# A hybrid decoder layer on one core: the gate, and q beside k, projected in 512-column blocks

## The chip, the cores and the metric

The kernel runs on one core of a Trainium2 chip. The metric is the device time of one execution in microseconds (us). The core's engines are named as in the profile: PE (matmul), PEld (its weight loads), DVE (VectorE), ACT (ScalarE), POOL (GpSimd) and SP (the queue that issues most transfers).

## The reference

One layer over 512 tokens of width 1024, all float32:

```python
h = rms_norm(x, norm_mix_w)
proj = h @ w_in                       # 1024 x 5664
z, xbc, dt_raw, q, k, v, f_raw = jnp.split(proj, [...], axis=-1)
y_ssd = ssd_mixer(xbc, z, dt_raw, ...)        # Mamba-2 scan, 16 heads, 2 groups, 4 chunks of 128 tokens
y_fox = fox_mixer(q, k, v, f_raw, ...)        # forgetting attention, 16 heads of 64, q and k normed per head
x = x + concat([y_ssd, y_fox]) @ w_out        # 2048 x 1024
hf = rms_norm(x, norm_ffn_w)
x = x + conv_gated_mlp(hf, w_up, ..., w_down) # 1024 x 5632, causal conv, silu gate, 2816 x 1024
```

In `ssd_mixer` the result of the scan is multiplied by silu(z), the gate, and normed per group of 512 columns. z, q, k and v have 1024 columns each.

## The kernel before

Every float32 matmul is done as three: each operand is split into a high part and a low part, and `mm3` adds high*high, high*low and low*high into one PSUM tile. `load_split` brings 128x1024 weights (512 KB, tile `wraw`, by SP), casts them on ACT to the high part `wh` (line 105) and subtracts on DVE or POOL for the low part `wl` (line 106). The table `LOW_PART` says which of the two engines does it for which block ("d" DVE, "p" POOL; a block without an entry goes to POOL). There are five `wraw` buffers and three of `wh` and of `wl`.

The normed input stands in SBUF as `xh` and `xl`, features on the partitions. The xBC columns are projected by `feature_tile` (weights stationary, 512 tokens moving; outputs called g and j in the trace). z, q, k and v are projected by `token_block`: 128 tokens of `xh` or `xl` are the stationary operand and 256 columns of the weights move. One call makes 256 output columns for all four token blocks, in two PSUM tiles of 512 columns (two token blocks side by side), with two loads of weights, each used for all four token blocks and then let go. That is 8 k-tiles x 4 token blocks x 3 = 96 matmuls of 256 columns a call. z takes two calls for each of two groups, q, k and v one call each for each of four head groups: 4 + 12 = 16 calls and 1536 matmuls, which the trace calls pq.

PSUM has three banks for such tiles (`bank`, pool pg), four for others (`mbank`), and one for po.

After a z call ACT reads each token block's 256 columns twice (a scaled copy to `gz`, line 392, and a tanh, line 393), and DVE multiplies. After a q or k call ACT makes a scaled copy `tok` (line 478) and a square (line 480), DVE sums the squares per head (line 481), POOL takes the power -1/2 for the norm (line 124), and DVE multiplies all of `tok` (line 486).

`ssd_scan` goes through four chunks of 128 tokens for each group. Per chunk: load and exponentiate the decay matrix `sc` (eight exponentials on ACT, line 427), multiply by C*B, make the output y and the next state, then multiply by the gate, norm, transpose (yT, line 464) and split y into `msh` and `msl`. Scan, and the steps of the attention heads (`fox_qk`, `fox_probs`, `fox_values`, 16 heads), are traced under high priority; the projections and output projections (`out_proj`, trace name po) fill in between. The list `fillers` gives at which head they are traced: q and k of group 1 at head 0, of group 2 at head 4, of group 3 at head 8, each used two heads later.

A scheduler orders the instructions of every engine ahead of time from priority, order of tracing and readiness in its own model of time; on the chip every queue then runs in that fixed order.

Behind the attention come the second norm, the up projection (trace name up, 44 feature tiles of 24 matmuls), and the down projection, seven block products with tiles called Y, X and Z. These use the same `wraw`, `wh` and `wl` buffers; in the down projection one of the operands (`oxh`) lies in the place of `xh`.

Of the kernel before, what the change touches and what calls it, by code (L numbers as in the profile page):

```python
# [8 lines left out]
F32 = mybir.dt.float32  # L9
# [47 lines left out]
def tile_hybrid_layer(  # L57
# [7 lines left out]
    wqkv: bass.AP,  # L65
# [34 lines left out]
    def load_split(src, sub=None):  # L100
        r = wp.tile([P, 1024], F32, tag="wraw", name="wraw", bufs=5)
        nc.sync.dma_start(r, src)
        h = wp.tile([P, 1024], F32R, tag="wh", name="wh", bufs=3)
        l = wp.tile([P, 1024], F32R, tag="wl", name="wl", bufs=3)
        act.copy(h, r)  # L105
        (sub or dve).tensor_tensor(out=l, in0=r, in1=raw(h), op=ALU.subtract)  # L106
        return h, l
# [55 lines left out]
    first = [wp.tile([P, 1024], F32R, tag=t, name=t, bufs=3) for t in ("wh", "wl")]  # L163
# [158 lines left out]
    def token_block(src, key="tb", behind=None):  # L322
        tiles = [bank("pq") for _ in range(2)]
        for kh in range(2):
            h, l = load_split(src[kh], sub=low_part(key))
            for b in range(2):
                for j in range(4):
                    k = 4 * kh + j
                    for c in range(2):
                        tb = 2 * b + c  # L330
                        s = slice(tb * P, (tb + 1) * P)
                        mm3(
                            tiles[b][:, c * 256 : (c + 1) * 256], xh[:, k, s], xl[:, k, s],
                            h[:, j * 256 : (j + 1) * 256], l[:, j * 256 : (j + 1) * 256],
                            k == 0 and c == 0, k == NK - 1, grouped=False,
                        )
                if behind is not None:
                    behind(2 * kh + b)
        return tiles

    def ssd_proj(g):
# [41 lines left out]
        for half in range(2):  # L383
            tiles = token_block(
                wz[2 * g + half], "z%d" % g,
                lambda piece: to_tokens(*late.pop(0)) if 4 * half + piece in (1, 3, 5 if g else 6) else None,
            )
            for tb in range(NTB):
                o = tiles[tb // 2][:, (tb % 2) * 256 : (tb % 2 + 1) * 256]
                dst = gz[tb][:, half * 256 : (half + 1) * 256]  # L390
                th = pss.tile([P, 256], F32, tag="th", name="th", bufs=2)
                act.activation(dst, o, AF.Copy, scale=rhalf[:, tb : tb + 1])
                act.activation(th, o, AF.Tanh, scale=rhalf[:, tb : tb + 1])
                dve.scalar_tensor_tensor(out=dst, in0=th, scalar=1.0, in1=dst, op0=ALU.add, op1=ALU.mult)
# [8 lines left out]
    def ssd_scan(g, x_tok, bT, cT, b_tok, gz):  # L403
# [5 lines left out]
        state = None  # L409
        for c in range(NTB):  # L410
# [5 lines left out]
            pool.tensor_tensor(out=heads(xdt), in0=heads(x_tok[c]), in1=per_head(tokS[:, 0, c, hs]), op=ALU.mult)  # L416
            if c < NTB - 1:
                dte = pss.tile([P, 2, HPG], F32, tag="dte", name="dte", bufs=2)
                dve.tensor_sub(dte[:, 0, :], last, tokS[:, 1, c, hs])
                dve.tensor_copy(dte[:, 1, :], last)  # L420
                act.activation(dte, dte, AF.Exp)
# [8 lines left out]
            dve.tensor_mul(sc, sc, cb[:, None, :P].broadcast_to([P, HPG, P]))  # L430
            yd = mbank("yd")
# [11 lines left out]
            if c < NTB - 1:  # L443
                dve.tensor_mul(heads(xdt), heads(xdt), per_head(dte[:, 0, :]))
                st = mbank("st")
                pe.matmul(st, b_tok[:, c, :], xdt, start=True, stop=True)
                new = pss.tile([P, 512], F32, tag="state", name="state", bufs=2)
                if state is None:
                    dve.tensor_copy(new, st)
                else:  # L450
                    pool.tensor_tensor(out=heads(new), in0=heads(state), in1=per_head(dte[:, 1, :]), op=ALU.mult)
                    dve.tensor_add(new, st, new)
                state = new
            dve.tensor_mul(y, y, gz[c])
# [4 lines left out]
            dve.scalar_tensor_tensor(  # L459
                out=y, in0=y, scalar=ss, in1=nwb, op0=ALU.mult, op1=ALU.mult  # L460
            )
# [5 lines left out]
            dve.tensor_sub(ml[:, :, s], tv, raw(mh[:, :, s]))  # L467
        return [(mh[:, j, :], ml[:, j, :]) for j in range(4)]
# [3 lines left out]
    def qk_proj(gi, t):  # L472
        tiles = token_block(wqkv[gi, t], "qk%d" % gi)
        tok = pa.tile([P, NTB, 256], F32, tag="tok", name="tok", bufs=4)
        ms = pa.tile([P, 16], F32, tag="ms", name="ms", bufs=2)
        for tb in range(NTB):
            o = tiles[tb // 2][:, (tb % 2) * 256 : (tb % 2 + 1) * 256]
            act.activation(tok[:, tb, :], o, AF.Copy, scale=r[:, tb : tb + 1])
            sq = pa.tile([P, 256], F32, tag="sq", name="sq", bufs=2)
            act.activation(sq, o, AF.Square, scale=r[:, tb : tb + 1])  # L480
            dve.tensor_reduce(
                out=ms[:, tb * 4 : tb * 4 + 4], in_=sq.rearrange("p (a b) -> p a b", b=HD), op=ALU.add, axis=AX.X
            )
        rsqrt(ms, ms, 1.0 / HD, 16)
        tv = tok.rearrange("p t (h d) -> p (t h) d", d=HD)
        dve.tensor_mul(tv, tv, ms[:, :, None].broadcast_to([P, 16, HD]))
        return tok

    def v_proj(gi):
        tiles = token_block(wqkv[gi, 2], "v%d" % gi)  # L490
# [137 lines left out]
    def project(g):  # L628
        qk[g] = [qk_proj(g, 0), qk_proj(g, 1)]
# [60 lines left out]
    nw = pa.tile([P, D], F32, tag="tok", name="nw", bufs=4)  # L690
    nc.sync.dma_start(nw, norm_ffn_w.to_broadcast([P, D]))
    for half in range(2):
        c = slice(half * 512, (half + 1) * 512)
        ks = slice(half * 4, half * 4 + 4)
        for tb in range(NTB):
            s = slice(tb * P, (tb + 1) * P)
            with urgent():
                xw = pa.tile([P, 512], F32, tag="tok", name="xw", bufs=4)
                (dve if (half, tb) == (1, 3) else pool).tensor_tensor(out=xw, in0=x2[:, tb, c], in1=nw[:, c], op=ALU.mult)
                t = mbank("hT")  # L700
                for j in range(4):
                    pe.transpose(t[:, j * P : (j + 1) * P], xw[:, j * P : (j + 1) * P], ident)
                tv = t.rearrange("p (j f) -> p j f", j=4)
                act.copy(hh[:, ks, s], tv)
                dve.tensor_sub(hl[:, ks, s], tv, raw(hh[:, ks, s]))
# [27 lines left out]

    def load_unit(q, u):
        rw = wp.tile([P, 1024], F32, tag="wraw", name="wraw", bufs=5)
# [23 lines left out]
    def up_proj(fs, cuts):  # L759
        ws = [load_split(wup[f]) for f in fs]  # L760
# [172 lines left out]
def _lay_out(i, np):  # L933
# [6 lines left out]
    def taps(v):  # L940
# [23 lines left out]
        "wz": w_in[:, 0:1024].reshape(2, 4, 128, 4, 256).transpose(3, 0, 2, 1, 4).reshape(4, 2, 128, 1024),  # L964
        "wxbc": _feature(w_in[:, 1024:2560], np),
        "wqkv": w_in[:, 2576:5648].reshape(2, 4, 128, 3, 4, 256).transpose(4, 3, 0, 2, 1, 5).reshape(4, 3, 2, 128, 1024),
# [29 lines left out]
```

## Time and profile before

| | |
|---|---|
| median of 3 runs | 812.52 us (810.81 to 813.75) |
| profiled execution, its own time | 812.5 us |
| its span in the trace | 810.7 us |
| PE busy | 800.7 us |
| DVE, ACT, POOL busy | 608.0, 437.7, 257.0 us |

The span is what the trace covers; 1.8 us of the execution's time lie around it. A matmul's end in the trace is modelled, and matmuls overlap, so the spacing of their starts says more than their durations. Engines other than PE run beside it.

### The profile page before, as it was taken

What the parts mean: (1) busy time and instruction counts of PE and PEld (TensorE: products, weight loads), DVE (VectorE), ACT (ScalarE), POOL (GpSimd) and SP (SyncE); (2) the same over time, 40 slices, a digit from 0 to 9 for tenths busy, and PEclk for the clock granted to TensorE, in tenths of its full rate; (3) what the DMA queues carried; (4) which work ended last, traced back from release to release, by engine and by line L of the source; (5) the groups of instructions that cost most, each with busy time, mean ns of one, the idle gap of its engine ahead of it and who ended that gap; (6) DMA issues with size and microseconds to landing.
All of it is one profiled execution on the core that took longest, in us unless ns stands there. A gap on an engine that the chain in (4) does not pass through costs nothing.

```text
span 810.7 us, 12402 instructions
## 1 busy us (share of the span) xinstructions
PE 800.7 (99%) x4591; PEld 697.2 (86%) x4591; DVE 608.0 (75%) x992; ACT 437.7 (54%) x835; POOL 257.0 (32%) x263
## 2 busy tenths in 40 slices
PE   8999999999999999999999999999999999999997
PEld 6899889988999999998888888888888888888886
DVE  4696898576579999998896867676667666777844
ACT  7466555543376977575664464344434433556531
POOL 0003344642265454234301423333322333133120
PEclk9999999999999999999999999999999999999999
DMA  9524222331343333334231263322332233299982
GB/s 326 207 94 135 104 104 80 118 130 52 105 131 104 105 106 117 105 108 127 66 89 69 78 183 104 103 86 96 105 103 83 100 103 89 84 252 196 215 190 92
DMA packets 31404, 98.22 MB, mean 121 GB/s; under 512 B 4016, under 2 KB 5104, under 8 KB 31344
## 3 DMA queue, kind: packets, MB, share of 16 engines
q1 hardware_dynamic: 27456, 85.38, 32.5%
q0 software_dynamic: 3456, 11.54, 8.0%
q8 instruction: 36, 0.59, 0.3%
q10 hardware_dynamic: 432, 0.52, 0.2%
q14 instruction: 24, 0.20, 0.1%
HBM read 91.56 MB, written 2.20 MB: 116 GB/s over the span
## 4 chain that ended last, share of the span: by engine, by line
PE 87%; DVE 4%; DMA 3%; POOL 2%; issue 2%; ACT 1%; SPq 0%; DVEq 0%; POOLq 0%
PE up L112 30%; PE pq L112 19%; PE po L112 10%; PE Y L112 6%; PE X L112 4%; PE Z L112 4%; PE g L112 3%; PE o L602 2%; PE pT L588 2%; PE j L112 1%; PE yd L433 1%; DMA sc<-cs_d 1%; PE S L562 1%; PE S L561 1%; DVE xs L375 1%
## 5 line engine op out<-in xcount | busy, mean ns | idle before, releaser
L105 ACT CAST wh<-wraw 128x1024 fp32r<-128x1024 f32 x103 | 108.4, 1052 | 134.3 <-PE up L112 78.6
L112 PE MATMUL pq<-wh,xl 128*128 128x256 f32 x512 | 147.5, 288 | 0.0
L112 PE MATMUL pq<-wh,xh 128*128 128x256 f32 x512 | 147.4, 288 | 0.0
L112 PE MATMUL pq<-wl,xh 128*128 128x256 f32 x512 | 146.2, 285 | 0.0
L112 PE MATMUL up<-hl,wh 128*128 128x512 f32 (+1 forms) x368 | 140.0, 381 | 0.0
L112 PE MATMUL up<-hh,wh 128*128 128x512 f32 (+1 forms) x368 | 139.9, 381 | 0.0
L112 PE MATMUL up<-hh,wl 128*128 128x512 f32 (+1 forms) x368 | 139.7, 380 | 0.0
L106 DVE TENSOR_TENSOR wl<-wraw,wh 128x1024 fp32r<-128x1024 f32 x86 | 110.2, 1281 | 25.3 <-ACT wh L105 21.3
L112 PEld LDWEIGHTS pq<-wh,xh 128*128 128x128 f32 x512 | 97.6, 191 | 2.0 <-issue 1.4
L112 PEld LDWEIGHTS pq<-wh,xl 128*128 128x128 f32 x512 | 97.6, 191 | 1.4 <-issue 1.2
L112 PEld LDWEIGHTS pq<-wl,xh 128*128 128x128 f32 x512 | 97.6, 191 | 1.3 <-issue 0.7
L112 PEld LDWEIGHTS up<-hl,wh 128*128 128x128 f32 x368 | 69.2, 188 | 13.4 <-issue 0.2
L112 PEld LDWEIGHTS up<-hh,wh 128*128 128x128 f32 x368 | 69.1, 188 | 13.2 <-issue 0.2
L112 PEld LDWEIGHTS up<-hh,wl 128*128 128x128 f32 x368 | 69.2, 188 | 13.1
L790 DVE TENSOR_TENSOR up<-up,R 128x512 f32<-128x512 f32 x44 | 30.3, 691 | 59.5 <-PE up L112 59.5
L795 DVE SCALAR_TENSOR_TENSOR ua<-up,pc,ua 128x511 f32<-128x511 f32 (+1 forms) x88 | 66.3, 758 | 1.4
L106 POOL TENSOR_TENSOR wl<-wraw,wh 128x1024 fp32r<-128x1024 f32 x17 | 42.1, 2474 | 59.8 <-ACT wh L105 56.2
L567 ACT ACTIVATE prob<-prob,nm 128x128 f32<-128x128 f32 (+1 forms) x64 | 35.8, 561 | 27.7 <-DVE nm L563 27.5
L751 ACT CAST wh<-T 128x1024 fp32r<-128x1024 f32 (+1 forms) x30 | 29.3, 976 | 36.9 <-PE Z L112 15.3
L752 DVE TENSOR_TENSOR wl<-T,wh 128x1024 fp32r<-128x1024 f32 (+1 forms) x30 | 33.8, 1134 | 19.2 <-ACT wh L751 18.8
L548 POOL TENSOR_SCALAR bias<-cum,tokS 128x256 f32<-128x256 f32 (+1 forms) x32 | 25.9, 818 | 67.9 <-DVE nm L563 59.5
L805 POOL TENSOR_TENSOR ua<-ua 128x512 f32<-128x512 f32 x11 | 15.0, 1364 | 92.6 <-DVE ua L795 92.6
(236 smaller groups left out, 1836.6 us busy)
## 6 DMA issues: line engine op xcount, KB each, us to landing
wraw<-in_wup_dram SPq DMA_DIRECT2D x44, 512.0 KB, 3.3
wraw<-in_wqkv_dram SPq DMA_DIRECT2D x24, 512.0 KB, 3.3
T<-in_wdown_dram POOLq DMA_DIRECT2D x20, 512.0 KB, 7.5
wraw<-in_wout_dram SPq DMA_DIRECT2D x16, 512.0 KB, 3.3
wraw<-in_wxbc_dram SPq DMA_DIRECT2D x11, 512.0 KB, 3.7
T<-in_wdown_dram SPq DMA_DIRECT2D x10, 512.0 KB, 5.9
wraw<-in_wdown_dram SPq DMA_DIRECT2D x10, 512.0 KB, 3.7
wraw<-in_wz_dram SPq DMA_DIRECT2D x8, 512.0 KB, 4.5
```

The costliest lines, as they stand in the source:

```text
L105: act.copy(h, r)
L106: (sub or dve).tensor_tensor(out=l, in0=r, in1=raw(h), op=ALU.subtract)
L112: ins = pe.matmul(o, a, b, start=start and n == 0, stop=stop and n == 2, **kw)
L548: (dve if qb == 2 else pool).tensor_scalar(out=b, in0=cum[:, :n], scalar1=-1.0, scalar2=edge, op0=ALU.mult, op1=ALU.add)
L567: act.activation(p, p, AF.Exp, scale=-1.0, bias=nm[:, qb : qb + 1], accum_out=sm[:, qb : qb + 1])
L588: pe.transpose(t[:, w : w + P], prob[:, o : o + P], ident)
L602: pe.matmul(cols[:m], v[:, kb, lh, vc], pt[:, s], start=kb == 0 and n == 0, stop=kb == NTB - 1, skip_group_check=True,)
L751: act.copy(h[:, :n], src[:, :n])
L752: dve.tensor_tensor(out=l[:, :n], in0=src[:, :n], in1=raw(h[:, :n]), op=ALU.subtract)
L790: dve.tensor_mul(xp, o, R2)
L795: dve.scalar_tensor_tensor(out=a[:, s:], in0=xp[:, : SEQ - s], scalar=pc[:, cw + 2 - s : cw + 3 - s], in1=a[:, s:], op0=ALU.mult, op1=ALU.add,
L805: pool.tensor_tensor(out=k, in0=k, in1=val, op=ALU.mult)
```

## The change

- A new `wide_block` replaces `token_block` for z and for q with k: 512 columns of weights move past each stationary 128 tokens (all 512 z columns of a group; 256 of q beside 256 of k). It makes two passes, each over two token blocks, one PSUM tile of 512 columns per token block. Its four loads are split once in the first pass and held for the second. v stays in `token_block`.
- What reads the results does so once per token block with 512 columns in place of twice with 256. The two norms of q and k follow when the whole block is done. `sq` has one buffer of 512 columns for two of 256.
- `wh` and `wl` get a fourth buffer, in pool pa, taken by every fourth load; `wraw` has three buffers for five, except in the down projection, where two more lie in pool pb. The up projection uses the three `wh` and `wl` of wp alone.
- In `ssd_scan`, the loading and the scores of chunk c+1 are traced ahead of gate, norm and transposes of chunk c.
- Tiles `nw` and `xw` of the second norm move to places in pool pf. The weights in memory are laid out for the new blocks.

```diff
         taken[key] = n + 1
         return dve if order[n % len(order)] == "d" else pool
 
-    def load_split(src, sub=None):
-        r = wp.tile([P, 1024], F32, tag="wraw", name="wraw", bufs=5)
+    loads = [0]
+
+    def load_split(src, sub=None, four=True):
+        r = wp.tile([P, 1024], F32, tag="wraw", name="wraw", bufs=3)
         nc.sync.dma_start(r, src)
-        h = wp.tile([P, 1024], F32R, tag="wh", name="wh", bufs=3)
-        l = wp.tile([P, 1024], F32R, tag="wl", name="wl", bufs=3)
+        where = pa if four and loads[0] % 4 == 3 else wp
+        loads[0] += 1
+        h = where.tile([P, 1024], F32R, tag="wh", name="wh", bufs=3 if where is wp else 1)
+        l = where.tile([P, 1024], F32R, tag="wl", name="wl", bufs=3 if where is wp else 1)
         act.copy(h, r)
         (sub or dve).tensor_tensor(out=l, in0=r, in1=raw(h), op=ALU.subtract)
         return h, l
...
 
     px_ctx = ExitStack()
     px = px_ctx.enter_context(tc.tile_pool(name="px", bufs=1))
-    first = [wp.tile([P, 1024], F32R, tag=t, name=t, bufs=3) for t in ("wh", "wl")]
+    first = [pa.tile([P, 1024], F32R, tag=t, name=t, bufs=1) for t in ("wh", "wl")]
     wdt = px.tile([P, NK, 64], F32R, tag="wdt", name="wdt")
...
         act.activation(eacs, tokS[:, 1, :, 0:16], AF.Exp)
         nc.sync.dma_start(dsk, ssd_d[0:1, :].to_broadcast([P, SSD_HEADS]))
 
-    def token_block(src, key="tb", behind=None):
+    def token_block(src, key="tb"):
         tiles = [bank("pq") for _ in range(2)]
         for kh in range(2):
             h, l = load_split(src[kh], sub=low_part(key))
...
                             h[:, j * 256 : (j + 1) * 256], l[:, j * 256 : (j + 1) * 256],
                             k == 0 and c == 0, k == NK - 1, grouped=False,
                         )
+        return tiles
+
+    def wide_block(src, key, use, behind=None):
+        ws = []
+        for b in range(2):
+            tiles = [bank("pw") for _ in range(2)]
+            for kq in range(4):
+                if b == 0:
+                    ws.append(load_split(src[kq], sub=low_part(key)))
+                h, l = ws[kq]
+                for j in range(2):
+                    k = 2 * kq + j
+                    for c in range(2):
+                        s = slice((2 * b + c) * P, (2 * b + c + 1) * P)
+                        cols = slice(j * 512, (j + 1) * 512)
+                        mm3(tiles[c], xh[:, k, s], xl[:, k, s], h[:, cols], l[:, cols], k == 0, k == NK - 1)
                 if behind is not None:
-                    behind(2 * kh + b)
-        return tiles
+                    behind(4 * b + kq)
+            for c in range(2):
+                use(2 * b + c, tiles[c])
 
...
             dve.scalar_tensor_tensor(out=dst, in0=xp, scalar=1.0, in1=dst, op0=ALU.add, op1=ALU.mult)
             if j < 10:
                 late.append((j, dst))
-        for half in range(2):
-            tiles = token_block(
-                wz[2 * g + half], "z%d" % g,
-                lambda piece: to_tokens(*late.pop(0)) if 4 * half + piece in (1, 3, 5 if g else 6) else None,
-            )
-            for tb in range(NTB):
-                o = tiles[tb // 2][:, (tb % 2) * 256 : (tb % 2 + 1) * 256]
-                dst = gz[tb][:, half * 256 : (half + 1) * 256]
-                th = pss.tile([P, 256], F32, tag="th", name="th", bufs=2)
-                act.activation(dst, o, AF.Copy, scale=rhalf[:, tb : tb + 1])
-                act.activation(th, o, AF.Tanh, scale=rhalf[:, tb : tb + 1])
-                dve.scalar_tensor_tensor(out=dst, in0=th, scalar=1.0, in1=dst, op0=ALU.add, op1=ALU.mult)
+
+        def gate(tb, o):
+            th = tmp("t", "th")
+            act.activation(gz[tb], o, AF.Copy, scale=rhalf[:, tb : tb + 1])
+            act.activation(th, o, AF.Tanh, scale=rhalf[:, tb : tb + 1])
+            dve.scalar_tensor_tensor(out=gz[tb], in0=th, scalar=1.0, in1=gz[tb], op0=ALU.add, op1=ALU.mult)
+
+        wide_block(
+            wz[g], "z%d" % g, gate,
+            lambda piece: to_tokens(*late.pop(0)) if piece in (1, 3, 5 if g else 6) else None,
+        )
         return x_tok, bT, cT, b_tok, gz
...
         hs = slice(g * HPG, (g + 1) * HPG)
         nwb = pss.tile([P, 512], F32, tag="nwb", name="nwb", bufs=1)
         nc.sync.dma_start(nwb, ssd_norm_w[0:1, g * 512 : (g + 1) * 512].to_broadcast([P, 512]))
-        state = None
-        for c in range(NTB):
+        def scores(c):
             s = slice(c * P, (c + 1) * P)
             sc = pss.tile([P, HPG, P], F32, tag="sc", name="sc", bufs=2)
             nc.sync.dma_start(sc, cs_d[None, c * 32 + g * HPG : c * 32 + (g + 1) * HPG, :].to_broadcast([P, HPG, P]))
             last = sc[:, :, P - 1]
             xdt = pss.tile([P, 512], F32, tag="xdt", name="xdt", bufs=2)
             pool.tensor_tensor(out=heads(xdt), in0=heads(x_tok[c]), in1=per_head(tokS[:, 0, c, hs]), op=ALU.mult)
+            dte = None
...
             cb = mbank("cb")
             pe.matmul(cb[:, :P], bT[:, s], cT[:, s], start=True, stop=True)
             dve.tensor_mul(sc, sc, cb[:, None, :P].broadcast_to([P, HPG, P]))
+            return sc, xdt, dte
+
+        def chunk(c, state, sc, xdt, dte):
+            s = slice(c * P, (c + 1) * P)
             yd = mbank("yd")
...
                     pool.tensor_tensor(out=heads(new), in0=heads(state), in1=per_head(dte[:, 1, :]), op=ALU.mult)
                     dve.tensor_add(new, st, new)
                 state = new
+            return y, state
+
+        def gated_norm(c, y):
+            s = slice(c * P, (c + 1) * P)
             dve.tensor_mul(y, y, gz[c])
             ss = pss.tile([P, 1], F32, tag="ss", name="ss", bufs=2)
             t = tmp("yt", "yt")
             act.activation(t, y, AF.Square, accum_out=ss)
             rsqrt(ss, ss, 1.0 / 512, 1)
-            dve.scalar_tensor_tensor(
-                out=y, in0=y, scalar=ss, in1=nwb, op0=ALU.mult, op1=ALU.mult
-            )
+            dve.scalar_tensor_tensor(out=y, in0=y, scalar=ss, in1=nwb, op0=ALU.mult, op1=ALU.mult)
             tp = mbank("yT")
             for j in range(4):
                 pe.transpose(tp[:, j * P : (j + 1) * P], y[:, j * P : (j + 1) * P], ident)
             tv = tp.rearrange("p (j f) -> p j f", j=4)
             act.copy(mh[:, :, s], tv)
             dve.tensor_sub(ml[:, :, s], tv, raw(mh[:, :, s]))
+
+        state, ahead = None, scores(0)
+        for c in range(NTB):
+            y, state = chunk(c, state, *ahead)
+            if c < NTB - 1:
+                ahead = scores(c + 1)
+            gated_norm(c, y)
         return [(mh[:, j, :], ml[:, j, :]) for j in range(4)]
...
-    def qk_proj(gi, t):
-        tiles = token_block(wqkv[gi, t], "qk%d" % gi)
-        tok = pa.tile([P, NTB, 256], F32, tag="tok", name="tok", bufs=4)
-        ms = pa.tile([P, 16], F32, tag="ms", name="ms", bufs=2)
-        for tb in range(NTB):
-            o = tiles[tb // 2][:, (tb % 2) * 256 : (tb % 2 + 1) * 256]
-            act.activation(tok[:, tb, :], o, AF.Copy, scale=r[:, tb : tb + 1])
-            sq = pa.tile([P, 256], F32, tag="sq", name="sq", bufs=2)
+    def qk_proj(gi):
+        tok = pa.tile([P, 2, NTB, 256], F32, tag="tok", name="tok", bufs=2)
+        ms = pa.tile([P, 2, NTB, 4], F32, tag="ms", name="ms", bufs=2)
+
+        def take(tb, o):
+            ov = o.rearrange("p (t f) -> p t f", t=2)
+            act.activation(tok[:, :, tb, :], ov, AF.Copy, scale=r[:, tb : tb + 1])
+            sq = pa.tile([P, 512], F32, tag="sq", name="sq", bufs=1)
             act.activation(sq, o, AF.Square, scale=r[:, tb : tb + 1])
             dve.tensor_reduce(
-                out=ms[:, tb * 4 : tb * 4 + 4], in_=sq.rearrange("p (a b) -> p a b", b=HD), op=ALU.add, axis=AX.X
+                out=ms[:, :, tb, :], in_=sq.rearrange("p (t a b) -> p t a b", t=2, b=HD), op=ALU.add, axis=AX.X
             )
-        rsqrt(ms, ms, 1.0 / HD, 16)
-        tv = tok.rearrange("p t (h d) -> p (t h) d", d=HD)
-        dve.tensor_mul(tv, tv, ms[:, :, None].broadcast_to([P, 16, HD]))
-        return tok
+
+        wide_block(wqk[gi], "qk%d" % gi, take)
+        for t in range(2):
+            mt = ms[:, t].rearrange("p a b -> p (a b)")
+            rsqrt(mt, mt, 1.0 / HD, 16)
+            tv = tok[:, t].rearrange("p t (h d) -> p (t h) d", d=HD)
+            dve.tensor_mul(tv, tv, mt[:, :, None].broadcast_to([P, 16, HD]))
+        return tok[:, 0], tok[:, 1]
 
     def v_proj(gi):
-        tiles = token_block(wqkv[gi, 2], "v%d" % gi)
+        tiles = token_block(wv[gi], "v%d" % gi)
...
 
     hh = pxt.tile([P, NK, SEQ], F32R, tag="xh", name="hh")
     hl = pxt.tile([P, NK, SEQ], F32R, tag="xl", name="hl")
-    nw = pa.tile([P, D], F32, tag="tok", name="nw", bufs=4)
+    nw = pf.tile([P, 1280], F32, tag="bias", name="nw", bufs=2)[:, :D]
     nc.sync.dma_start(nw, norm_ffn_w.to_broadcast([P, D]))
     for half in range(2):
         c = slice(half * 512, (half + 1) * 512)
...
         for tb in range(NTB):
             s = slice(tb * P, (tb + 1) * P)
             with urgent():
-                xw = pa.tile([P, 512], F32, tag="tok", name="xw", bufs=4)
+                xw = pf.tile([P, 512], F32, tag="osum" if tb % 2 else "cum", name="xw", bufs=2)
...
     def part(q, u):
         return wdown[q, :, UNITS[u][0] * 512 : UNITS[u][1] * 512]
 
+    raws = [0]
+
     def load_unit(q, u):
-        rw = wp.tile([P, 1024], F32, tag="wraw", name="wraw", bufs=5)
+        where = wp if raws[0] % 5 < 3 else pb
+        raws[0] += 1
+        rw = where.tile([P, 1024], F32, tag="wraw", name="wraw", bufs=3 if where is wp else 2)
         nc.sync.dma_start(rw[:, 0 : (UNITS[u][1] - UNITS[u][0]) * 512], part(q, u))
         return rw
...
     R2 = pu.tile([P, SEQ], F32, tag="R2", name="R2")
 
     def up_proj(fs, cuts):
-        ws = [load_split(wup[f]) for f in fs]
+        ws = [load_split(wup[f], four=False) for f in fs]
         os = [bank("up") for _ in fs]
...
-        "wz": w_in[:, 0:1024].reshape(2, 4, 128, 4, 256).transpose(3, 0, 2, 1, 4).reshape(4, 2, 128, 1024),
+        "wz": w_in[:, 0:1024].reshape(4, 2, 128, 2, 512).transpose(3, 0, 2, 1, 4).reshape(2, 4, 128, 1024),
         "wxbc": _feature(w_in[:, 1024:2560], np),
-        "wqkv": w_in[:, 2576:5648].reshape(2, 4, 128, 3, 4, 256).transpose(4, 3, 0, 2, 1, 5).reshape(4, 3, 2, 128, 1024),
+        "wqk": w_in[:, 2576:4624].reshape(4, 2, 128, 2, 4, 256).transpose(4, 0, 2, 1, 3, 5).reshape(4, 4, 128, 1024),
+        "wv": w_in[:, 4624:5648].reshape(2, 4, 128, 4, 256).transpose(3, 0, 2, 1, 4).reshape(4, 2, 128, 1024),
```

## Rows read from the trace of the kernel before

**Rows 1.** The page's part 1: span, busy time (share), instructions.
```profile
span 810.7 us, 12402 instructions
...
PE 800.7 (99%) x4591; PEld 697.2 (86%) x4591; DVE 608.0 (75%) x992; ACT 437.7 (54%) x835; POOL 257.0 (32%) x263
```
**Rows 2.** The page's part 2: busy tenths and granted PE clock in 40 slices.
```profile
PE   8999999999999999999999999999999999999997
...
PEclk9999999999999999999999999999999999999999
```
**Rows 3.** The page's part 4: the chain that ended last, by engine.
```profile
PE 87%; DVE 4%; DMA 3%; POOL 2%; issue 2%; ACT 1%; SPq 0%; DVEq 0%; POOLq 0%
```
**Rows 4.** Waits of PE behind its start: line, releaser, us in total, times, longest.
```profile
PE S L561 <- DMA ks<-ks: 1.2, 2, 0.7
...
PE yT L464 <- DVE y L459: 0.6, 1, 0.6
PE xT L352 <- ACT x_tok L358: 0.5, 1, 0.5
...
PE po L112 <- DVE x L258: 0.3, 1, 0.3
```
**Rows 5.** The chain in order of time, unbroken matmul stretches: start, us, what, count.
```profile
145.53 10.43 PE pq L112 x87
156.62 3.83 PE pq L112 x32
...
366.30 9.81 PE po L112 x42
...
475.24 225.78 PE up L112 x996
...
730.97 15.01 PE Z L112 x66
```
**Rows 6.** Groups by form, one of three alike: count, busy us, mean ns, idle before.
```profile
L112 PE MATMUL pq<-wh,xl 128*128 128x256 f32 x512 | 147.5, 288 | 0.0
```
**Rows 7.** Timeline of PE behind transposes, eight starts apart: start, us, what.
```profile
103.35 0.40 PE L112 MATMUL g<-xh,wl 128*128 128x512 f32 x1
...
105.20 0.39 PE L112 MATMUL g<-xl,wh 128*128 128x512 f32 x1
```
**Rows 8.** Groups by form: readers of PSUM on ACT, and two DVE steps of q and k.
```profile
L590 ACT CAST ph<-pT 128x512 fp32r<-128x512 f32 x32 | 17.8, 585 | 6.9 <-PE pT L588 5.7 <-PE o L602 1.0
...
L478 ACT ACTIVATE tok<-pq,r 128x256 f32<-128x256 f32 x32 | 15.1, 472 | 4.2 <-PE pq L112 4.0
...
L486 DVE TENSOR_TENSOR tok<-tok,ms 128x1024 f32<-128x1024 f32 x8 | 13.7, 1710 | 0.5 <-POOL ms L124 0.4
...
L481 DVE TENSOR_REDUCE ms<-sq 128x4 f32<-128x256 f32 x32 | 12.9, 414 | 5.1 <-ACT sq L480 4.8
```
**Rows 9.** Groups by form: the two steps of a split, and where DVE or POOL does it.
```profile
L106 DVE TENSOR_TENSOR wl<-wraw,wh 128x1024 fp32r<-128x1024 f32 x86 | 110.2, 1281 | 25.3 <-ACT wh L105 21.3 <-PE rbc L145 3.8
L105 ACT CAST wh<-wraw 128x1024 fp32r<-128x1024 f32 x103 | 108.4, 1052 | 134.3 <-PE up L112 78.6 <-PE po L112 22.0 <-issue 7.3
...
L106 POOL TENSOR_TENSOR wl<-wraw,wh 128x1024 fp32r<-128x1024 f32 x17 | 42.1, 2474 | 59.8 <-ACT wh L105 56.2 <-issue 2.9 <-POOL ss L124 0.7
```
**Rows 10.** The page's part 6: a load of weights, KB, us to landing.
```profile
wraw<-in_wqkv_dram SPq DMA_DIRECT2D x24, 512.0 KB, 3.3
```
**Rows 11.** Stretches of the attention: us, PE, PEld, DVE, ACT, POOL busy, clock, DMA, GB/s.
```profile
260.00:300.00 40.00, 39.92 (x326) 38.93 (x325) 37.48 (x94) 34.30 (x81) 19.53 (x27) 1.00 0.38 113
...
430.00:459.00 29.00, 28.69 (x147) 23.20 (x145) 19.73 (x30) 9.79 (x15) 10.59 (x8) 1.00 0.23 74
```
**Rows 12.** The chain in order of time: exponentials of a scan, and a norm of q or k.
```profile
79.62 2.44 ACT sc L427 x8
...
253.88 2.93 POOL ms L124
256.83 3.41 DVE tok L486
```

More of the change, by code (lines that the diff above doesn't have):

```diff
@@ L64, in tile_hybrid_layer @@
     wxbc: bass.AP,
-    wqkv: bass.AP,
+    wqk: bass.AP,
+    wv: bass.AP,
     wout: bass.AP,
@@ L628, in project @@
     def project(g):
-        qk[g] = [qk_proj(g, 0), qk_proj(g, 1)]
+        qk[g] = qk_proj(g)
     def project_v(g):
```

## The prediction

> **What bounds the kernel now.** I read the page's busy shares first: PE is busy 800.7 of 810.7 us, DVE 75%, ACT 54% [rows 1]. Busy PE alone would say little, since the ends of matmuls are modelled, so the slices come next: PE is at 9 in all but the first and last of them, and the granted clock stands at its upper level, 2.4 GHz, throughout [rows 2]. The chain that ended last gives PE 87% of the span [rows 3]. And the waits of PE behind its start sum to 1.2 + 0.6 + 0.5 + 0.3 = 2.6 us [rows 4]. So one queue, PE's, sets the time nearly everywhere; what counts is how far apart its matmuls start, and the other engines count only where they would make PE wait. A matmul taken off PE, or made cheaper there, comes off the end; less work elsewhere does not.
>
> **What a matmul costs.** Unbroken stretches of the chain give the spacing. 256 columns (pq): 10.43 / 87 = 0.1199 us and 3.83 / 32 = 0.1197, so 0.1198. 512 columns (up): 225.78 / 996 = 0.2267 [rows 5]. At 2.4 GHz, 256 and 512 columns alone would take 0.1067 and 0.2133 us; each matmul carries some 13 ns beside its columns. Two of 256 take 0.2396 us, one of 512 takes 0.2267.
>
> **The change, step by step.**
>
> Step 1, the matmuls. z is 4 calls of the old block, q and k 8: 12 x 96 = 1152 of the 1536 pq matmuls [rows 6] go, 1152 x 0.1198 = 138.0 us. 576 of 512 columns come. No 512-column matmul with `xh` stationary and weights moving is in the trace, so I bound it. Below: 0.2267, as in up, and as in the down projection's Z, whose stationary operand lies in the place of `xh` and whose weights move (15.01 / 66 = 0.2274) [rows 5]. Above: 0.2336, from the output projection, also token blocks against moving weights (9.81 / 42) [rows 5]. The sum is 130.6 us below and 134.5 above; the gain is 7.4 or 3.5. Between them lies g just behind transposes, where the sequence has been broken: 8 starts in 105.20 - 103.35 = 1.85 us, 0.2313 each [rows 7]. I take 0.2267 for the half that runs in long stretches (z and the first q/k block, 288 matmuls, 65.3 us) and 0.2313 for the other three q/k blocks, which the attention heads break up (288, 66.6 us): 131.9, a gain of 6.1 us.
>
> Step 2, reading the results. 16 + 16 readings of z and 32 + 32 of q and k by ACT, at some 472 ns, become 48 of 512 columns. The nearest row, a 512-column cast out of PSUM, took 585 ns [rows 8]. ACT goes from some 45 to some 28 us. The 32 sums of squares on DVE at 414 ns become 16 of 414 to 828 ns: 0 to 6.6 us less. Neither engine sets the end, so I count nothing.
>
> Step 3, banks. There are still three banks, but a pass now ends with both its tiles 3 matmuls apart. The next pass writes its first tile in the third bank and its second in the bank of the first tile just finished. From that tile's last matmul to the first one that wants its bank there are 6 matmuls, 6 x 0.2267 = 1.36 us; two ACT readings take 2 x 0.585 = 1.17 [rows 8]. This fits if ACT is free, and the second pass has other work ready: all its weights are split already, so the first tile's 24 matmuls (5.4 us) can go ahead. I count nothing; the price without that cover is the third rival.
>
> Step 4, weights. In a first pass a load serves 12 matmuls, 2.7 us, where it served 48 of 256 columns, 5.8 us, before; in a second pass none is needed. A buffer comes free every 2.7 us of the second pass, so the first is free 8.2 us before the block ends. A cast takes 1.05 and the low part 1.28 on DVE or 2.47 on POOL [rows 9], 2.3 to 3.5 us together: hidden for three buffers, and the fourth is wanted only 8.2 us into the next block. The landing, 3.3 us [rows 10], is hidden while three raw buffers run ahead. A feature tile of the up projection lasts 24 x 0.2267 = 5.4 us, so three raw buffers suffice there too. If this cover were gone, one late split at each of the six wide blocks would cost up to 6 x 3.5 = 21 us; nothing in the rows asks for it.
>
> Step 5, the norms of q and k. They come in one piece when a block ends: the power on POOL took 2.93 us and the multiplication on DVE 3.41 in one place of the chain [rows 12], where its mean is 1.71 [rows 8]. Now two of each stand there. They are used two heads later, and PE has v and output projections to fill with. Counted at nothing; the second rival prices it.
>
> Step 6, the scan. The scores of the next chunk move ahead of gate and norm of this one on ACT (the eight exponentials took 2.44 us [rows 12]), DVE and POOL; SP's order of loads does not change, as the norm issues none. yT may come later, but only the output projection wants it, and that is traced behind the q/k block. The two waits of PE that this could remove are 0.6 and 0.5 us [rows 4], and it could add the like: nothing.
>
> Step 7, `nw` and `xw` in other places: their buffers are let go when heads 14 and 15 are done, before x2 is. Nothing.
>
> Sum: 812.5 us (the profiled execution, equal to the median; its span is 1.8 less) - 6.1 = 806.4.
>
> **A rule that speaks against it.** The rows say some 13 ns per matmul beside its columns [rows 5]. The Trainium skill (TensorE: Matmul & The Clock Gate, "Wait — 56ns, not 53.3ns?") puts that fixed cost at about 2.5 ns; an estimate from its figure is 2.5 ns for each pair merged, 576 x 2.5 = 1.4 us, and the kernel would end at 811.1. The trace does not agree where stretches are long; its nearest approach is the output projection, below.
>
> **Rivals.**
>
> First, the cost goes with the columns: the new matmuls run at the output projection's 0.2336 [rows 5], nearly twice the 0.1198 of half the width. Gain 3.5, time 809.0, and with one or two new microseconds of waiting no change that can be measured. For it: operands of the same kind, and many short stretches. Against: Z, with the same place stationary, took 0.2274. The skill's rule of the paragraph above points the same way. 0.14.
>
> Second, the attention cannot use what PE saves. DVE is busy 37.48 of 40 us from 260 to 300, where q and k of group 1 are projected, though only 19.73 of 29 at the end [rows 11]. The fox half of the gain, 288 x (0.2396 - 0.2313) = 2.4 us, goes, giving 808.8; if each of three blocks also shows one more multiplication at its mean of 1.71 us [rows 8], 5.1 in all, 813.9. 0.14.
>
> Third, and slower: the bank of step 3. Six blocks have 12 ends of passes. With one cast of 1.05 us [rows 9] ahead of the two readings on ACT, which takes its queue in order, the bank is free 1.17 + 1.05 - 1.36 = 0.86 us late; behind eight exponentials [rows 12], 2.3 us. 12 x 0.86 = 10.3 us gives 816.7. It decides from 6.1 / 12 = 0.5 us per end. For it: the room shrinks from 48 matmuls of 256 columns, 5.8 us. Against: in 16 blocks PE never waited for ACT to read a projection [rows 4], and the order is laid out with readiness in view. 0.15.
>
> **How the numbers follow.** My forecast has 0.57, the three rivals 0.14, 0.14 and 0.15. A measurement of this kernel can tell about 0.3%, 2.4 us, from no change. Faster: the forecast, half of the first rival and 0.06 of the second, 0.70. Same: the rest of those two, 0.15. Slower: the third, 0.15. The range starts at 802.0: the whole 7.4, the 2.6 of waits, and half a microsecond. It ends at 812.0, which holds the first rival with new waits and most of the second, and leaves out the third.
>
> **What would show it.** 192 matmuls of each of the three kinds with 512 columns, spaced 0.2267 (step 1; 0.2336 for the first rival), and the up projection's long stretch beginning near 469 where it began at 475.24 [rows 5], with the same length. New rows of PE waiting on ACT's readings would be the third rival; waits of transposes on DVE in the attention the second. I would be wrong if the stretch from 475 on changed its length, or if PE waited for `wh` or `wl` at the start of a block.

## The result and the profile after

The changed kernel takes 807.4 us (median of 6 runs, 805.41 to 808.07) where the kernel before takes 811.66 us beside it (6 runs): ratio 0.9942, 95% interval 0.9925 to 0.996. The profiled execution took 807.45 us, its span is 805.7. The forecast was 806.4 in 802.0 to 812.0. One execution below, 2835.54 us in experiment 1, stands apart from all the others and is left out of its median.

Parts 1, 2 and 4 of the page after, which answer to [rows 1 to 3]:

```profile
span 805.7 us, 11156 instructions
...
PE 794.8 (99%) x4015; PEld 665.2 (83%) x4015; DVE 605.7 (75%) x968; ACT 430.0 (53%) x787; POOL 263.8 (33%) x263
...
PE   8999999999999999999999999999999999999997
...
PEclk9999999999999999999999999999999999999999
...
PE 90%; DVE 6%; DMA 2%; issue 1%; POOL 0%; ACT 0%; SPq 0%; DVEq 0%
```

PE has 576 instructions fewer and 5.9 us less of busy time; the span is 5.0 us shorter. DVE and ACT lost 2.3 and 7.7 us; PE is still the chain, and experiment 1, which keeps their lighter load, loses the gain.

Waits of PE after, behind its start (answer to [rows 4]):

```profile
PE po L117 <- DVE x L263: 0.8, 2, 0.5
PE pT L626 <- DVE pl L629: 0.7, 1, 0.7
PE po L117 <- ACT mfh L650: 0.6, 1, 0.6
PE yT L491 <- DVE y L488: 0.5, 1, 0.5
```

Their sum, 2.6 us, is that of before, in other places. None is for a reading of a `pw` bank, and none for `wh` or `wl` at the start of a wide block.

The chain after in order of time: start, us, what, count (answer to [rows 5]):

```profile
58.63 5.54 PE pw L117 x24
65.06 4.61 PE pw L117 x20
...
138.24 7.11 PE pw L117 x31
...
146.01 6.25 PE pw L117 x27
...
153.99 5.77 PE pw L117 x25
...
363.46 11.10 PE po L117 x48
...
469.69 225.79 PE up L117 x996
...
725.45 14.99 PE Z L117 x66
```

The first two `pw` stretches belong to the gate of group 0 and are spaced 5.54 / 24 = 0.2308 and 4.61 / 20 = 0.2305 us. The other three (the end of group 1's gate, then the first q/k block) are spaced 7.11 / 31 = 0.2294, 6.25 / 27 = 0.2315 and 5.77 / 25 = 0.2308 us, together 19.13 / 83 = 0.2305. The up projection begins at 469.69, 5.55 us earlier than in [rows 5], and its long stretch has the same length. Behind it 0.55 us is given back: from 469.69 to the end of the span are 336.0 us, before 335.5.

Groups by form after (answers to [rows 6] and [rows 8]):

```profile
L117 PE MATMUL pw<-wh,xh 128*128 128x512 f32 x192 | 76.9, 406 | 0.0
...
L512 ACT ACTIVATE tok<-pw,r 128x512 f32<-128x512 f32 x16 | 11.0, 688 | 0.4 <-PE pw L117 0.3
...
L515 DVE TENSOR_REDUCE ms<-sq 128x8 f32<-128x512 f32 x16 | 10.9, 681 | 3.0 <-ACT sq L514 3.0
```

An ACT reading of 512 columns takes some 688 ns, where I had put the 585 of a cast; all 48 take 33.0 us, where I had 28.

### The profile page after: what moved, and what is told of

It reads as the page before. It is cut to its first block, busy times and chain, and to the rows that moved or that the text cites. A ratio compares the mean times of both kernels' runs of the same rounds, so it can differ in the third digit from the quotient of the medians.

```text
span 805.7 us, 11156 instructions
## 1 busy us (share of the span) xinstructions
PE 794.8 (99%) x4015; PEld 665.2 (83%) x4015; DVE 605.7 (75%) x968; ACT 430.0 (53%) x787; POOL 263.8 (33%) x263
## 4 chain that ended last, share of the span: by engine, by line
PE 90%; DVE 6%; DMA 2%; issue 1%; POOL 0%; ACT 0%; SPq 0%; DVEq 0%
PE up L117 30%; PE pw L117 16%; PE po L117 10%; PE Y L117 6%; PE g L117 5%; PE X L117 4%; PE Z L117 4%; PE pq L117 3%; PE o L640 2%; PE pT L626 2%; PE yd L458 2%; PE j L117 1%; PE S L599 1%; PE S L600 1%; DVE xs L397 1%
## 5 line engine op out<-in xcount | busy, mean ns | idle before, releaser
L117 PE MATMUL pw<-wh,xh 128*128 128x512 f32 x192 | 76.9, 406 | 0.0
L117 PE MATMUL pw<-wl,xh 128*128 128x512 f32 x192 | 76.1, 396 | 0.0
L117 PE MATMUL pw<-wh,xl 128*128 128x512 f32 x192 | 75.7, 396 | 0.0
L586 POOL TENSOR_SCALAR bias<-cum,tokS 128x256 f32<-128x256 f32 (+1 forms) x32 | 22.1, 700 | 83.6 <-DVE nm L601 67.8
L117 PEld LDWEIGHTS pw<-wl,xh 128*128 128x128 f32 x192 | 36.2, 188 | 7.3 <-issue 0.7
L117 PEld LDWEIGHTS pw<-wh,xh 128*128 128x128 f32 x192 | 36.1, 188 | 7.3 <-issue 0.5
L117 PEld LDWEIGHTS pw<-wh,xl 128*128 128x128 f32 x192 | 36.1, 188 | 7.1
```

What stands on the lines that cost most here:

```text
L117: ins = pe.matmul(o, a, b, start=start and n == 0, stop=stop and n == 2, **kw)
L586: (dve if qb == 2 else pool).tensor_scalar(out=b, in0=cum[:, :n], scalar1=-1.0, scalar2=edge, op0=ALU.mult, op1=ALU.add)
```

## The experiments

All ratios are against the kernel before in the same call. A time that I give without more is a median.

**1. Only the width undone.** Tiles, passes, readings, loads and the scan's order of the changed kernel stay; each matmul of 512 columns becomes two of 256.

```diff
-cols = slice(j * 512, (j + 1) * 512)
-mm3(tiles[c], xh[:, k, s], xl[:, k, s], h[:, cols], l[:, cols], ...)
+for q in (0, 256):
+    cols = slice(j * 512 + q, j * 512 + q + 256)
+    mm3(tiles[c][:, q : q + 256], xh[:, k, s], xl[:, k, s], h[:, cols], l[:, cols], ...)
```

> The changed kernel with each of its 576 new matmuls of 512 columns made as two of 256, everything else (four loads held, two passes, readers of 512 columns, scan order, buffers) as changed. Theory (the gain is the fixed cost of a matmul on PE): in unbroken stretches two of 256 cost 2 x 0.1194 and one of 512 costs 0.2299 us in the changed kernel's trace, so 576 x 0.0089 = 5.1 us come back: 812 to 813 us, no different from the kernel before. Rival (the gain is the lighter load of ACT and DVE, the fourth weight buffer or the new order of the scan): it stays near 807.5.

Measured: 811.84 us, ratio 0.9994 [0.9983, 1.0006]. The chain of this run:

```profile
142.20 8.12 PE pw L117 x68
...
476.55 225.78 PE up L117 x996
```

8.12 / 68 = 0.1194 us a half, 0.2388 a pair, against 0.2305 for one of 512. With the width the whole gain goes: 811.84 - 807.4 = 4.4 us, or 4.4 / 576 = 7.7 ns for each pair merged; the spacing alone gives 576 x (0.2388 - 0.2305) = 4.8. The instructions are also laid out anew, with one wait of PE for a norm, 1.3 us, that the changed kernel lacks, so the 4.4 is not spacing to the last tenth. With matmuls of 256 columns the rest of the change, in sum, is worth nothing. The Trainium skill (TensorE: Matmul & The Clock Gate, "Wait — 56ns, not 53.3ns?") has 2.5 ns for this; the runs do not agree.

**2. Only the scan's order undone.** The changed kernel, with gate, norm and transposes of a chunk traced ahead of the next chunk's scores again.

```diff
 for c in range(NTB):
     y, state = chunk(c, state, *ahead)
+    gated_norm(c, y)
     if c < NTB - 1:
         ahead = scores(c + 1)
-    gated_norm(c, y)
```

> The changed kernel with the scores of the next chunk traced behind gate and norm again, as before. Theory (prediction, step 6): the waits of PE that this order moves are 0.5 to 0.6 us each, so 806 to 809 us, no measurable difference to the changed kernel. Rival (the scan order carries a good part of the gain): 809.5 us or more.

Measured: 829.9 us, ratio 1.02 [1.0178, 1.0223]. I had expected next to nothing; it is 22.5 us over the changed kernel. Stretches of this run (us, PE, PEld, DVE, ACT, POOL busy, clock, DMA, GB/s):

```profile
290.00:300.00 10.00, 8.12 (x62) 7.04 (x60) 9.80 (x25) 7.69 (x17) 6.11 (x11) 1.00 0.44 130
300.00:310.00 10.00, 9.21 (x38) 7.28 (x39) 8.61 (x25) 6.11 (x19) 2.41 (x6) 0.66 0.29 82
310.00:320.00 10.00, 5.11 (x31) 4.00 (x30) 9.74 (x23) 8.71 (x21) 2.37 (x6) 0.86 0.28 77
320.00:330.00 10.00, 10.00 (x48) 8.62 (x47) 8.13 (x21) 4.59 (x14) 2.06 (x5) 0.80 0.13 29
...
420.00:470.00 50.00, 45.59 (x222) 36.22 (x221) 37.80 (x80) 24.34 (x51) 8.26 (x10) 0.93 0.21 64
```

From 290 to 330 PE idles 7.6 us (after: 0.9), and behind an idle stretch the granted clock stands partly at 1.2 GHz: 0.34 + 0.14 + 0.20 of 10 us are 6.8 us more. From 420 to 470 it is 4.4 us idle (0.9) and 0.07 of 50, 3.5 us, of clock. Excess in all 6.7 + 6.8 + 3.5 + 3.5 = 20.5 of the 22.8 us by which the spans differ (828.5 - 805.7). The place is the attention; what differs ahead of it is the scan: its last chunk was transposed at 242.9 us, and the attention's first transposes followed at once; after they stand at 212.9, before at 225.7. The projections that should fill the attention's gaps had been used up beside the longer scan. Counted in the traces in matmuls of 256 columns (one of 512 counts as two), the projections and output projections that still stand behind the attention's first transposes are 1206 here, 1453 after and 1372 before.

**3. Width undone in the old order**: the two edits above together, to tell the order alone from the order with wide blocks.

```diff
+for q in (0, 256):    # as in 1
...
+    gated_norm(c, y)    # as in 2
```

> The changed kernel with both the 512-column matmuls made as two of 256 (as in e1) and the old order of the scan (as in e2): two passes, held weights, wide readers and buffers stay. Theory W (e2 lost its 22 us because matmuls of 512 columns stand between the PE steps of a scan, about as many as of 256 before, so that each step waits longer and the attention starts at 243 in place of 226 us): the scan ends near 225 us again and the time is 811 to 815 us. Rival S (the blocks of two passes, with z's last token blocks ready late, hold up the scan whatever the width): the attention starts at 240 us or later and the time is 824 us or more.

Measured: 813.54 us, ratio 1.0016 [0.9997, 1.0034]; the scan ends at 229.3, and 1369 of the matmuls just counted are left behind it. Theory W holds, though the scan ends 4 us behind its 225, and rival S is out. So the old order costs 813.54 - 811.84 = 1.7 us with matmuls of 256 columns and 22.5 with 512. How, shows in the chain of the scan. First run 3, then run 2 (`cb` is a step of the scan on PE, `yd` its next one, `pw` the filling between them):

```profile
144.15 0.22 PE cb L454 x2
144.37 3.81 PE pw L117 x32
148.18 1.73 PE yd L462 x16
...
159.03 0.22 PE cb L454 x2
159.25 3.81 PE pw L117 x32
163.06 1.73 PE yd L462 x16
```

```profile
126.52 0.22 PE cb L450 x2
...
126.85 6.03 PE pw L117 x26
132.88 1.73 PE yd L458 x16
...
145.31 0.22 PE cb L450 x2
145.54 5.77 PE pw L117 x25
151.31 1.73 PE yd L458 x16
```

With the old order the layout puts 25 or 26 wide fillers between the two steps where it put 32 narrow ones, not half as many, so `yd` stands some 2 us later. From the first `yT` to the last are 141 us in run 2 and 127 in run 3: 14 us over the seven chunks between them, 2 us each. The kernel before has 127, too, the changed one 112. Why the layout counts fillers so was not tried.

**4. The scan's new order alone**, in the kernel before: its scan is cut into the three functions of the diff and traced in their order, nothing else.

```diff
-for c in range(NTB):
+state, ahead = None, scores(0)
+for c in range(NTB):
+    y, state = chunk(c, state, *ahead)
+    if c < NTB - 1:
+        ahead = scores(c + 1)
+    gated_norm(c, y)
```

> The kernel before with nothing changed but the order of the scan (scores of the next chunk traced ahead of gate and norm). Theory (the order matters only once the blocks between the scan's steps are wide): PE has 2.6 us of waits behind its start in the kernel before, so no more can be gained: 810 to 813 us. Rival (the new order pays by itself, as the attention can start earlier): 809.5 us or less.

Measured: 816.33 us, ratio 1.0038 [1.0017, 1.0058]: slower by itself. Timeline of POOL and of DVE (start, us, what), then two stretches:

```profile
115.99 2.34 POOL L106 TENSOR_TENSOR wl<-wraw,wh 128x1024 fp32r<-128x1024 f32 x1
```

```profile
116.06 2.82 DVE L467 SCALAR_TENSOR_TENSOR y<-y,ss,nwb 128x512 f32<-128x512 f32 x1 [0.45 <-POOL ss L124]
```

```profile
115.00:120.00 5.00, 1.96 (x14) 1.76 (x12) 4.55 (x4) 0.36 (x1) 3.33 (x2) 0.82 0.16 33
120.00:130.00 10.00, 10.00 (x49) 8.97 (x48) 8.90 (x14) 2.37 (x6) 2.47 (x2) 0.58 0.25 95
```

The norm's multiplication, 0.75 us in the median of its eight, took 2.82 while POOL split a weight; the transposes `yT` waited 3.0 us for it; PE was busy 1.96 of 5 us, and then the granted clock averaged 0.58 over 10 us, partly at 1.2 GHz. Idle and clock are 3.0 + 0.9 + 4.2 = 8.1 us in 15; this profiled execution, 818.73 us, is the longest of the twelve (813.28 to 818.73), so the median lost less there. The Trainium skill (GPSIMD Engine Reference, "1. Specifications") says that the two engines share their way into SBUF when a DVE instruction has two inputs there, which the trace fits. In the changed kernel there is also the other sequence, and the one that began first was not slowed: a split on DVE from 241.56 us took 1.23 us, no more than its mean of 1.29, though one on POOL began at 242.03; that one took 3.02, where the mean there is 2.49.

**5. That one split moved to DVE**, everything else as in run 4.

```diff
-    "z1": "pdpd",
+    "z1": "pddd",
```

> The kernel before with the new scan order alone, as two runs ago (816.33 us), but the third weight split of group 1's gate is done by DVE and no longer by POOL. In that run the split on POOL (115.99 to 118.33 us) lay over DVE's norm multiplication, which took 2.82 us and not 0.75, the transposes yT waited 3.0 us for it, and the granted clock then stood at the lower level in part of 115 to 130 us. Theory P (the loss of the new scan order alone is this one collision and what it sets off): the multiplication is back at 0.75 us, the wait of yT below 1.5 us, the clock at 1.00 through 110 to 140 us, and the time is 810 to 813 us, no more than the kernel before. Rival R (the order itself is worse with narrow blocks): DVE has 1.2 us more in the same place, the wait stays at 2 to 3 us or turns up elsewhere, and the time stays at 815 us or more.

Measured: 812.67 us, ratio 1.0011 [0.9999, 1.0023]. The same instruction and stretches:

```profile
117.20 0.75 DVE L467 SCALAR_TENSOR_TENSOR y<-y,ss,nwb 128x512 f32<-128x512 f32 x1 [0.45 <-POOL ss L124]
```

```profile
115.00:120.00 5.00, 3.96 (x35) 3.75 (x34) 4.55 (x8) 1.64 (x6) 2.40 (x3) 1.00 0.23 85
120.00:130.00 10.00, 10.00 (x75) 8.96 (x75) 9.71 (x16) 4.50 (x11) 1.42 (x1) 1.00 0.29 107
```

The multiplication is back at 0.75 us, the wait is 1.0 there, the clock 1.00, and the time lies in the range given for the collision as cause. So the new order by itself gains and loses nothing. Against the kernel before in its own call run 4 lost 816.33 - 812.28 = 4.1 us and this run 812.67 - 811.46 = 1.2; the difference, 2.9 us, is the price of one collision and what it set off. (The edit moves some other instructions on DVE and PE too, so this size is rough.) What a collision costs depends on what PE has to do meanwhile. The changed kernel has one as long:

```profile
141.75 2.89 DVE L488 SCALAR_TENSOR_TENSOR y<-y,ss,nwb 128x512 f32<-128x512 f32 x1 [1.65 <-POOL ss L129]
```

It lies beside the `pw` stretch from 138.24 to 145.35 us, and PE did not wait.

**6. z alone wide, and q with k alone wide**, both in the new order: in the changed kernel one of the two goes back to `token_block` with its old readers.

```diff
-wide_block(wqk[gi], "qk%d" % gi, take)                       # z alone wide
+tiles = token_block(wqkv[gi, t], "qk%d" % gi)
...
-wide_block(wz[g], "z%d" % g, gate, ...)                      # q and k alone wide
+tiles = token_block(wz[2 * g + half], "z%d" % g, ...)
```

> The changed kernel with q and k projected in 256-column blocks as before; z stays wide, scan order and buffers stay. Theory (the gain is the fixed cost of a matmul, 0.0089 us for each pair merged, on average over long and broken stretches): z has 192 of the 576 pairs, 1.7 us of gain against the kernel before: 809.5 to 811 us. Rival (the gain comes mostly from z, whose stretches are long and whose readers are fewer, or from the scan order): 808 us or less.

> The changed kernel with z projected in 256-column blocks as before; q beside k stays wide, scan order and buffers stay. Theory (fixed cost of a matmul): q and k have 384 of the 576 pairs, 3.4 us of gain against the kernel before: 807.5 to 809.5 us. Rival (in the attention PE's saving is lost, as DVE is busy 37.5 of 40 us there): 811 us or more.

Measured: 814.89 us, ratio 1.0022 [1.0002, 1.0043], and 815.61 us, ratio 1.0031 [1.0012, 1.0051]. Neither is the part of the gain that I expected; both are slower than before. The largest waits of PE with z alone, then with q and k alone:

```profile
PE qkT L546 <- DVE tok L519: 2.7, 1, 2.7
PE S L594 <- DVE x L262: 1.5, 1, 1.5
```

```profile
PE yT L494 <- DVE y L491: 2.6, 1, 2.6
PE S L602 <- DMA ks<-ks: 1.5, 1, 1.5
```

With z alone the wait of 2.7 us is a collision again, first POOL, then DVE:

```profile
260.89 2.79 POOL L110 TENSOR_TENSOR wl<-wraw,wh 128x1024 fp32r<-128x1024 f32 x1
```

```profile
261.38 3.38 DVE L519 TENSOR_TENSOR tok<-tok,ms 128x1024 f32<-128x1024 f32 x1
```

In the changed kernel this multiplication takes 1.28 us in the mean. The 3.41 us of the same step in [rows 12] and the wait of 1.3 us in experiment 1 are such collisions too (splits on POOL from 256.77 and from 266.96 us). With q and k alone PE was idle 2.6 us between 115 and 130, and the clock there averaged 0.77, another 0.23 x 15 = 3.5. This is the place of run 4, but not its cause: the multiplication took its usual 0.74 us and stood behind other work of DVE. Each variant is laid out anew, and each order brings its own one or two waits of 1.5 to 2.7 us, together as large as the gain in question, so these two runs can't say how the gain divides between z and q with k.

**7. Where operands lie.** `pw` ran at 0.2305, not 0.2267. Two explanations: broken sequences, or the places of the operands, as `xh` and three of the four weight buffers start 64 bytes past a multiple of 128 and the fourth, in pa, at a multiple. An unused tile of 64 bytes was put first into pool pa (first run), first into the pool of `xh` (second), and ahead of the constants (third). The third run has this one tile, not the two that its expectation names: it moves all that lies behind the constants, weights and `xh` alike, by 64 bytes.

```diff
+dve.memset(pxt.tile([P, 16], F32, tag="pad", name="pad"), 0.0)   # second run
```

> The changed kernel with 64 bytes put in front of pool pa, so that the fourth weight buffer and the operands of the output projection start at the same residue of their address modulo 128 bytes (64) as xh and the other weight buffers; every engine's order stays. Theory A (512 columns cost 0.2267 us where the stationary and the moving tile have the same residue, 0.2333 where not): the new matmuls go from 0.2299 to 0.2267 or a little above (576 x 0.0032 = 1.8 us), the output projection from 0.2311 to 0.2267 (384 x 0.0044 = 1.7), the first projections from 0.2295 to 0.2275 (0.5): 803 to 804.5 us. Theory B (the slower spacing comes from sequences broken by transposes, as the prediction had it): no change, 806.5 to 808.5.

> The changed kernel with 64 bytes put in front of xh, so that xh (and hh and oxh in its place) and oh start at residue 0 modulo 128 bytes, while the three weight buffers of wp stay at 64 (the fourth and the operands of the output projection go to 64). Theory A (equal residues are fast): up goes from 0.2267 to 0.2333 (1008 x 0.0066 = 6.7 us), Y, X and Z likewise (468 x 0.0064 = 3.0), the first projections (1.2) and the new matmuls (2.0) too, and the output projection gains 1.7: about 818 to 819 us. Theory B (residues don't matter): 806.5 to 808.5.

> The changed kernel with one unused 64-byte tile ahead of the constants and one ahead of the pool of xh, so that the weights' splits (wh, wl), xh and the output projection's oh all move by 64 bytes and keep their places to each other. Theory C (a matmul is dearer where its two operands stand 64 bytes apart from a multiple of 128, as xh against wh did when xh alone was moved): Y, X, Z and up keep the spacings of the changed kernel (0.2271 and 0.2267 us) and the time is 807 us. Theory A' (each operand's own place counts, whatever the other's): spacings of Y, X, Z move again, to 0.2333 or to below 0.2271, and the time differs by 2 us or more from 807.4 us.

Measured: 807.13 us, ratio 0.9935 [0.992, 0.9951]; 813.2, ratio 1.0013 [1.0, 1.0026]; 808.25, ratio 0.9957 [0.9941, 0.9972]. The chain in the second run, then in the third:

```profile
471.87 227.97 PE up L117 x996
...
730.64 15.40 PE Z L117 x66
```

```profile
469.75 225.78 PE up L117 x996
...
725.45 14.96 PE Z L117 x66
```

Moving `xh`'s pool alone makes Z 15.40 / 66 = 0.2333 (0.2271 after) and up 227.97 / 996 = 0.2289 (0.2267), and the kernel 5.8 us longer (less than Theory A's 818 to 819, as up stays below its 0.2333); moving the weights along brings both back. So it is the place of the two operands to each other that counts, and both kernels have the good one in the long stages. For `pw` it is not the explanation: its mean over the 480 distances between starts that are under 0.25 us is 0.2299 after, 0.2302 in the first run and 0.232 in the second. The output projection stays at 0.2305 in the first run (0.2311 after), where Theory A had 0.2267. Nor do interruptions explain all of it: the first ten distances behind one average 0.2302 us, the 141 later ones still 0.2290. Most of these stand at 0.227, but slower ones, up to 0.240, come back within a stretch of `pw` alone. Why stays open.

## Why the prediction was right

**Step 1** carries the result, as experiment 1 shows, and its mechanism holds: two matmuls of 256 columns cost more than one of 512. The cost beside the columns is not quite the same for each: 0.2305 is 17 ns over the 0.2133 of the columns alone, and 0.1194 is 13 ns over 0.1067. The size was a little high. 288 matmuls were to run at 0.2267; the z blocks and the first q/k block, which I had put there, run at 0.2294 to 0.2315 as well, and those of group 0 at 0.2308 and 0.2305, the first of them ahead of the scan's first step at 64.6 us. So my reason for the slower half, a sequence broken by other steps, explains a part at most (experiment 7). 576 x (2 x 0.1194 - 0.2299) = 5.1 us where I had 6.1; the profiled executions differ by 5.0 (812.5 - 807.45), the medians by 4.3.

**Steps 2 and 3.** Nothing for the end, as counted, though the margin that I gave for step 3 was none: two readings take 2 x 0.688 = 1.38 us, the six matmuls 1.36. No wait for ACT's reading shows all the same, and the third rival did not occur; that other work ready on PE covers it, as I had argued, was not tested.

**Steps 4, 5 and 7.** No wait for weights or norms; the loads and the long stages are as before. In step 5 the cover is thin: experiments 1 and 6 show waits of `qkT` on a norm, 1.3 and 2.7 us, in orders laid out a little differently, each where POOL splits a weight under the norm's multiplication. The clock, which I read as at its upper level throughout, averages 0.94 in the first 30 us of either kernel; as it is alike in both, nothing hangs on it.

**Step 6** was wrong in its reason. I looked at two waits of 0.6 and 0.5 us and counted the new order as nothing. With matmuls of 256 columns that is near enough (1.7 us gained in experiment 3, 1.2 lost in 5, more lost in 4 by a collision). With 512 it is worth 22.5 us: from the first `yT` to the last the scan takes 112 us and not 141, and the last `yT` comes at 212.8 and not at 242.9. Long fillers still stand in it (27 of them at 146.01 us); that scores and norm of two chunks now pass them side by side and no longer one behind the other is how I read the chain, and no run tests it by itself. Here the number is luck: it is right because both edits are in the change. Had only the wide block been made, a forecast by my steps would have missed by some 23 us (829.9 for 806.4), for a reason that was not among the rivals. The second rival is its nearest, an attention that cannot use what PE saves, but it priced DVE (808.8 to 813.9 us) and did not see that the fillers would be gone.

**First rival** (the cost goes with the columns): the time alone can't tell, as 807.4 us lies between the forecast's 806.4 and this rival's 809.0. The spacing speaks against it, 0.2305 and not 0.2336, though the output projection itself, 11.10 / 48 = 0.2313 now, shows how near the two are.

## What to carry to other kernels

Merging two matmuls of 256 columns into one of 512 bought some 8 ns a pair here, where the spacings of the long stages had promised 13; count it by start-to-start spacing in stretches like those where it will run. A longer matmul is also a longer unit of filling: where a serial chain takes its turns between fillers, price what the chain gains in length, and look at which filling is left for the stage behind it. And test an edit together with the order it was made for: undone or done alone, these parts came out from 22 us slower to no gain. Before a difference of a few us is put down to an edit, look whether a split on POOL has come to lie over a multiplication on DVE that PE waits for.

## What the runs showed of the hardware

- A weight split on POOL that began just ahead of a DVE multiplication: 2.82 us for 0.75, 2.89 in the changed kernel, 3.38 for 1.28 with z alone; gone where the split was moved (experiment 5). Where a split on DVE began 0.47 us ahead of one on POOL, POOL's took longer (3.02 us for 2.49) and DVE's did not (1.23 for 1.29).
- Stops of PE of 3.0 us (experiment 4) and 2.6 us (6, q and k alone) were followed by a lower granted clock, 0.58 over 10 us and 0.77 over 15; one of 2.7 us (6, z alone) and one of 1.0 us (5) were followed by 1.00. The length of the stop alone does not decide.
- 64 bytes between the places of two operands modulo 128: 0.2333 instead of 0.2271 us per matmul of 512 columns in the down projection, 0.2289 instead of 0.2267 in the up projection.
